# An output projection by one level of Strassen's algorithm, with sums of the weights made ahead of time on GpSimd

## The chip, the cores and the metric

The kernel runs on one core of one Trainium2 chip. The core has five engines with their own instruction streams: TensorE (PE, matmuls; PEld are its weight loads), VectorE (DVE), ScalarE (ACT), GpSimd (POOL) and SyncE (SP, which here issues all DMA transfers). The engines meet only through semaphores. The metric is the time of one execution on the device in microseconds (us); a lower one is better.

## The reference, cut to what matters

One layer of a hybrid decoder over 1024 positions of width 1024. The input is normalised and modulated, projected by w_in, and goes through three groups of heads (an mLSTM over chunks, a sliding-window attention, a stick-breaking attention), each gated by its own z. The three results stand side by side and are projected by w_out, normalised, gated and added to x:

```python
def rmsnorm(x, g):
    xf = x.astype(jnp.float32)
    y = xf * lax.rsqrt(jnp.mean(xf * xf, axis=-1, keepdims=True) + EPS)
    return (y * g.astype(jnp.float32)).astype(x.dtype)

def hybrid_layer(x, c_act, ...):
    mod = c_act @ w_mod + b_mod
    shift, scale, gate = jnp.split(mod, 3, axis=-1)
    h = rmsnorm(x, g_pre) * (1.0 + scale[:, None]) + shift[:, None]
    proj = h @ w_in
    ...
    y_m = mlstm_branch(mu, mv, mi, mf, ...) * jax.nn.silu(mz)
    y_a = swa_branch(aq, ak, av, a_sinks) * jax.nn.silu(az)
    y_s = stickbreak_branch(sq, sk, sv) * jax.nn.silu(sz)
    y = jnp.concatenate([y_m, y_a, y_s], axis=-1) @ w_out
    return x + gate[:, None] * rmsnorm(y, g_post)
```

All inputs are float32. y and w_out are 1024 x 1024.

## The kernel before, in words

Every product of float32 matrices is made of three matmuls on operands that are split in two: a high part (a cast to the type that PE reads, on ACT) and a low part (the difference, on DVE or POOL), joined as high·high + low·high + high·low. `split` does this. Tiles are 128 partitions by up to 512 columns, one PSUM bank.

The stages, in order: the modulation and the normalised h with the projection of the mLSTM's input; the convolution `cu` (until about 92 us); the gate chain, in which the mLSTM's gate values go through DRAM (`d_m`, `d_wi`) and, beside it, the row `gacc` = silu(c)·w_gate is summed from eight loads `wg` (`gate_row`, lines 528 to 540) and taken through PE (`gate_sum`, `gbps`, line 548); the m loop, eight chunks of the mLSTM (from about 160 us); the window attention; the stick-breaking attention; and the output projection (from 453 us). In all stages before the last, PE's idle time is filled with the projections by w_in: a `Filler` puts matmuls of the next projection (`pd`, `ptav`) between those of the stage. The result y is held transposed, in eight tiles of 128 of its columns (dst_j) by 1024 positions, in two halves of positions. `gated` multiplies each by its gate; the first six tiles are stored in DRAM as a high and a low part (`d_yh`, `d_yl`), the last two (`ys`) stay on the chip.

PE's instructions run in the order of the code. On the other engines a scheduler places them by priorities and by its own estimates, so that the order there is not that of the code. All loads and stores are in SP's one queue, in its order; each waits there for its semaphores, and what stands behind waits with it.

The output projection before: `wo_load` (lines 1078 to 1081) brings w_out in eight chunks of 512 KB and splits them; `y_load` brings the y parts back into hh and hl; then `out_mm` (lines 1104 to 1111) does three matmuls for each of 8 row tiles of 128 positions, 2 halves of 512 columns and 8 chunks k of 128. For the first four row tiles k is the outer loop, over eight PSUM banks. `out_fin` takes squares from PSUM on ACT, multiplies by the gate row `gbc` on DVE, makes the power on POOL and scales and adds x on DVE (lines 1122 to 1131).

## Time and profile before

| | us |
|---|---|
| median of 3 runs | 551.35 (551.1 to 551.76) |
| profiled execution | 551.07 |
| its span, first to last instruction | 549.3 |
| PE busy | 523.7 (95%) |
| DVE busy | 332.8 (61%) |
| ACT busy | 250.5 (46%) |
| POOL busy | 220.3 (40%) |
| output projection, first to last start of a matmul | 453.29 to 542.66 |
| mean granted PE clock, as a share | 0.999 |

The views give, for an instruction: its start and duration in us, the engine, the line of the kernel, the operation, the tile written and the tiles read, the shapes, and in brackets how long the engine had been idle before it and what released it. "x3" at the end of a row of a timeline stands for three alike, whose times are added. DMA issues are rows of SP's queue (SPq); their duration is that of the issue, not of the transfer.

### The profile page before, as it was taken

What the parts mean: (1) busy time and instruction counts of PE and PEld (TensorE: products, weight loads), DVE (VectorE), ACT (ScalarE), POOL (GpSimd) and SP (SyncE); (2) the same over time, 40 slices, a digit from 0 to 9 for tenths busy, and PEclk for the clock granted to TensorE, in tenths of its full rate; (3) what the DMA queues carried; (4) which work ended last, traced back from release to release, by engine and by line L of the source; (5) the groups of instructions that cost most, each with busy time, mean ns of one, the idle gap of its engine ahead of it and who ended that gap; (6) DMA issues with size and microseconds to landing.
All of it is one profiled execution on the core that took longest, in us unless ns stands there. A gap on an engine that the chain in (4) does not pass through costs nothing.

```text
span 549.3 us, 8550 instructions
## 1 busy us (share of the span) xinstructions
PE 523.7 (95%) x2953; PEld 448.3 (82%) x2953; DVE 332.8 (61%) x750; ACT 250.5 (46%) x571; POOL 220.3 (40%) x206
## 2 busy tenths in 40 slices
PE   4799999999999999999998999899999999999995
PEld 3577899999978989888786888788888888888884
DVE  4686692054726787678887489787868442118232
ACT  5643533361122333167587478667668332213111
POOL 2365765430023343244434348575666442111000
PEclk9999999999999999999999999999999999999999
DMA  8982361248986355699952488354421169607421
GB/s 299 417 308 71 116 233 51 58 146 237 279 247 209 107 159 138 162 277 269 235 178 88 145 225 248 134 153 154 135 78 58 39 201 401 239 1 243 141 85 68
DMA packets 63660, 96.57 MB, mean 176 GB/s; under 512 B 17601, under 2 KB 36993, under 8 KB 63489
## 3 DMA queue, kind: packets, MB, share of 16 engines
q1 hardware_dynamic: 63616, 96.03, 55.5%
q8 instruction: 23, 0.38, 0.3%
q14 instruction: 21, 0.16, 0.1%
HBM read 69.24 MB, written 25.20 MB: 172 GB/s over the span
## 4 chain that ended last, share of the span: by engine, by line
PE 79%; DVE 10%; DMA 3%; ACT 3%; issue 2%; SPq 1%; POOL 1%; DVEq 0%; POOLq 0%; ACTq 0%
PE pd L359 26%; PE ptav L385 6%; PE mu L233 6%; PE op L1111 5%; PE op L1110 5%; PE op L1109 5%; PE tp L996 3%; PE ptmif L385 2%; DVE cu L509 2%; DMA mbc<-d_m 2%; PE ops L1014 2%; PE ops L1015 2%; PE z L965 2%; PE mr L197 1%; PE z L966 1%
## 5 line engine op out<-in xcount | busy, mean ns | idle before, releaser
L359 PE MATMUL pd<-hh,wl_d 128*128 128x512 f32 x256 | 71.2, 400 | 0.0
L359 PE MATMUL pd<-hh,wh_d 128*128 128x512 f32 x256 | 70.6, 400 | 0.0
L359 PE MATMUL pd<-hl,wh_d 128*128 128x512 f32 x256 | 70.6, 398 | 0.0
L359 PEld LDWEIGHTS pd<-hh,wh_d 128*128 128x128 f32 x256 | 46.1, 188 | 8.4 <-issue 0.5
L359 PEld LDWEIGHTS pd<-hl,wh_d 128*128 128x128 f32 x256 | 46.1, 188 | 8.1
L302 POOL TENSOR_TENSOR wl_d<-w_d,wh_d 128x512 fp32r<-128x512 f32 x32 | 44.1, 1400 | 21.1 <-ACT wh_d L300 20.0
L359 PEld LDWEIGHTS pd<-hh,wl_d 128*128 128x128 f32 x256 | 45.8, 188 | 7.7
L1109 PE MATMUL op<-woh,hh 128*128 128x512 f32 x128 | 50.6, 396 | 0.0
L1110 PE MATMUL op<-woh,hl 128*128 128x512 f32 x128 | 50.6, 396 | 0.0
L1111 PE MATMUL op<-wol,hh 128*128 128x512 f32 x128 | 50.6, 396 | 0.0
L984 POOL TENSOR_TENSOR sg<-sg,pr 128x512 f32<-128x512 f32 (+1 forms) x30 | 31.1, 1043 | 20.8 <-DVE pr L982 20.6
L859 POOL TENSOR_SCALAR zb<-zb,mx 128x256 f32<-128x256 f32 (+1 forms) x24 | 21.6, 916 | 42.2 <-DVE mx L856 27.9
L70 ACT CAST ah<-tp 128x512 fp32r<-128x512 f32 (+2 forms) x56 | 24.3, 436 | 29.2 <-PE tp L996 21.2
L71 DVE TENSOR_TENSOR al<-tp,ah 128x512 fp32r<-128x512 f32 (+2 forms) x56 | 27.4, 493 | 16.9 <-ACT ah L70 16.4
L1122 ACT ACTIVATE sj<-op 128x512 f32<-128x512 f32 x16 | 9.5, 598 | 50.8 <-PE op L1111 48.3
L1110 PEld LDWEIGHTS op<-woh,hl 128*128 128x128 f32 x128 | 24.0, 188 | 5.9
L1111 PEld LDWEIGHTS op<-wol,hh 128*128 128x128 f32 x128 | 24.0, 188 | 5.8
L1109 PEld LDWEIGHTS op<-woh,hh 128*128 128x128 f32 x128 | 24.0, 188 | 5.7
L1126 POOL TENSOR_TENSOR st<-st,mhalf 128x1 f32<-128x1 f32 x8 | 4.9, 608 | 57.0 <-DVE st L1125 57.0
L849 ACT ACTIVATE zb<-zb,mx 128x256 f32<-128x256 f32 (+1 forms) x48 | 23.2, 486 | 7.3 <-DVE mx L838 7.3
L982 DVE TENSOR_TENSOR_SCAN pr<-z,mzero 128x128 f32<-128x128 f32 (+3 forms) x32 | 25.6, 814 | 0.4 <-ACT z L973 0.2
L971 ACT ACTIVATE sg<-z 128x512 f32<-128x512 f32 (+3 forms) x48 | 23.8, 495 | 1.3 <-PE z L968 1.1
(247 smaller groups left out, 1326.8 us busy)
## 6 DMA issues: line engine op xcount, KB each, us to landing
wm<-in_w_ss_dram SPq DMA_DIRECT2D x16, 512.0 KB, 7.8
w_d<-in_w_dm_dram SPq DMA_DIRECT2D x16, 512.0 KB, 3.7
xt<-in_x_dram SPq DMA_DIRECT2D x8, 512.0 KB, 8.3
wg<-in_w_gate_dram SPq DMA_DIRECT2D x8, 512.0 KB, 6.0
wo<-in_w_out_dram SPq DMA_DIRECT2D x8, 512.0 KB, 5.4
xr<-in_x_dram SPq DMA_DIRECT2D x8, 512.0 KB, 4.9
out_dram<-ot SPq DMA_DIRECT2D x16, 256.0 KB, 2.3
hh<-d_yh SPq DMA_DIRECT2D x12, 256.0 KB, 6.0
```

What stands on the lines that cost most here:

```text
L70: e_hi(dst_h, src)
L71: e_lo.tensor_tensor(out=dst_l, in0=src, in1=dst_h.bitcast(F32), op=ALU.subtract)
L233: T.matmul(mu_acc[j][n], w[:, cs], h[:, k, t], start=(k == 0 and w is wh and h is hh), stop=(k == KT - 1 and h is hl))
L302: G.tensor_tensor(out=wl[:, a:b], in0=z[:, a:b], in1=wh.bitcast(F32)[:, a:b], op=ALU.subtract)
L359: T.matmul(ps, w[:, k, :], h[:, k, t], start=(k == 0 and w is wh and h is hh), stop=(k == KT - 1 and h is hl))
L385: T.matmul(ps[:, 0:self.N], h[:, k, t], w[:, k % 2, :], start=(k == 0 and q == 0), stop=(k == KT - 1 and q == 2))
L971: A.activation(sg[:, 0:w], zps[:, 0:w], AF.Sigmoid)
L982: V.tensor_tensor_scan(out=rev(pr), data0=rev(zps), data1=mzero[:, 0:1].to_broadcast([P, w]), initial=1.0 if nxt is None else nxt, op0=ALU ...
L984: (G if w > 256 and (h > 0 or i > 3) else V).tensor_tensor(out=sg[:, 0:w], in0=sg[:, 0:w], in1=pr[:, 1:w + 1], op=ALU.mult)
L1109: T.matmul(o, hh[:, k, t], woh[:, k, cs], start=(k == 0), stop=False)
L1110: T.matmul(o, hl[:, k, t], woh[:, k, cs], start=False, stop=False)
L1111: T.matmul(o, hh[:, k, t], wol[:, k, cs], start=False, stop=(k == KT - 1))
```

## The change

The output projection becomes one level of Strassen's algorithm in Winograd's form. y and w_out are cut into quarters (positions by 512 for y, 512 by 512 for w_out). Seven products of quarters or sums of quarters take the place of eight. Each has 4 row tiles, 4 chunks of 128 and three matmuls of 128x512. Their names in the code are "11", "21", "t2", "t1", "22", "t3" and "t4", by the weights that they use, in this order. The weights t1 to t4 are sums of quarters of w_out; `w_sums` makes them in the gate chain's stage on POOL, in the room of the tile `mup` (the convolution's input, no longer needed there): for each of four chunks c it loads two rows of w_out (512 KB each), makes four differences, four casts and four low parts, and stores eight tiles of 256 KB in `d_th` and `d_tl`. The sums of y are made on DVE in the last stage (`y_ready`) from a third copy of y, `d_y`, in float32; `gated` now stores it for six tiles, and leaves out the split for the second half of four of them.

In `product` the row tile is the outer loop and the chunk the inner one. The results are added up in SBUF from PSUM by DVE (`e2` to `e4`); squares are now of the sum in SBUF. The x rows are loaded in halves. The loads of `bias_a`, `ka` and `va` (the window attention's) come after the work of w_sums on SP's queue.

The core of the diff:

```diff
+                store(d_y[dst_j, :, t], y)
+                if n == 1 and dst_j < 4:
+                    return
...
+    def w_sums():
+        room = mup.rearrange("p a b -> p (a b)")
+        z = room[:, 0:2 * D].rearrange("p (r a b) -> p r a b", r=2, a=2)
+        w11, w12, w21, w22 = z[:, 0, 0, :], z[:, 0, 1, :], z[:, 1, 0, :], z[:, 1, 1, :]
+        for c in range(4):
+            load(z[:, 0], w_out[c].rearrange("p (a b) -> p a b", a=2))
+            load(z[:, 1], w_out[4 + c].rearrange("p (a b) -> p a b", a=2))
+            for o, a, b in ((w11, w12, w11), (w12, w22, w12), (w22, w22, w11), (w21, w22, w21)):
+                G.tensor_tensor(out=o, in0=a, in1=b, op=ALU.subtract)
+            for m, (n, o) in enumerate(((0, w11), (2, w12), (1, w22), (3, w21))):
+                h = room[:, 2 * D + m % 2 * 512:2 * D + m % 2 * 512 + 512].bitcast(F32R)
+                split(h, o.bitcast(F32R), o, G.tensor_copy, G)
+                store(d_th[n, :, c, :], h)
+                store(d_tl[n, :, c, :], o)
...
     m_load(0)
+    w_sums()
...
-    woh = wop.tile([P, KT, D], F32R, name="woh")
-    wol = wop.tile([P, KT, D], F32R, name="wol")
-
-    def wo_load(k):
-        w = wop.tile([P, D], F32, tag="wo", bufs=2, name=f"wo{k}")
-        load(w, w_out[k])
-        split(woh[:, k, :], wol[:, k, :], w, A.copy, V if k % 2 else G)
...
+    def y_quarter(i, r, c):
+        if r == 1 and c >= 2:
+            return ys[:, c - 2, halves[i]]
+        if (i, r, c) in ahead:
+            return ahead.pop((i, r, c))
+        z = wop.tile([P, 512], F32, tag="yo", bufs=8, name=f"yo{i}{r}{c}")
+        load(z, d_y[4 * r + c][:, halves[i]])
+        return z
+    def w_pair(name):
+        wq_[name] = [wop.tile([P, 4, 512], F32R, tag=z, bufs=2, name=f"{z}{name}") for z in ("wqh", "wql")]
+        return wq_[name]
+    def w_ready(name, r, n):
+        h, l = w_pair(name)
+        for c in range(4):
+            z = wop.tile([P, 512], F32, tag="wo", bufs=4, name=f"wo{r}{n}{c}")
+            load(z, w_out[4 * r + c][:, halves[n]])
+            split(h[:, c, :], l[:, c, :], z, A.copy, V)
+    def t_ready(n):
+        h, l = w_pair(f"t{n}")
+        load(h, d_th[n - 1])
+        load(l, d_tl[n - 1])
+    def y_ready(i, r, chunk):
+        for c in range(4):
+            k = 4 * r + c
+            split(hh[:, k, halves[i]], hl[:, k, halves[i]], chunk(c), A.copy, V)
...
+    w_ready("11", 0, 0)
+    w_ready("21", 1, 0)
+    ahead.update({q: y_quarter(*q) for q in [(1, 0, 0), (1, 1, 0), (1, 0, 1), (1, 1, 1), (1, 0, 2), (1, 0, 3),
+                                             (0, 0, 0), (0, 0, 1)]})
     fill.through(I_SZ1)
     y_load(0)
-    for k in range(4, KT):
-        wo_load(k)
     fill.through(99)
     y_load(1)
+
...
+    def product(yi, yr, w, evac):
+        wh, wl = wq_[w]
+        ps = [fbank(f"p{w}_{i}") if i == 3 else ops_.tile([P, 512], F32, tag="op", name=f"p{w}_{i}")
+              for i in range(4)]
+        for i in range(4):
+            t = slice(yi * 512 + i * P, yi * 512 + (i + 1) * P)
+            for c in range(4):
+                k = 4 * yr + c
+                T.matmul(ps[i], hh[:, k, t], wh[:, c, :], start=(c == 0), stop=False)
+                T.matmul(ps[i], hl[:, k, t], wh[:, c, :], start=False, stop=False)
+                T.matmul(ps[i], hh[:, k, t], wl[:, c, :], start=False, stop=(c == 3))
+            evac(i, ps[i])
...
+    def square(src, i, n):
+        sj = op_.tile([P, 512], F32, tag="sj", bufs=2, name=f"sj{i}_{n}")
+        A.activation(sj, src, AF.Square, accum_out=st[:, i, n:n + 1])
+    def finish(i, parts):
+        xr = [wop.tile([P, 512], F32, tag="yo", bufs=8, name=f"xr{i}_{n}") for n in range(2)]
         for n in range(2):
+            load(xr[n], x[i * P:(i + 1) * P, halves[n]])
+        s_ = st[:, i, :]
+        V.tensor_scalar(out=s_[:, 2:3], in0=s_[:, 1:2], scalar1=s_[:, 0:1], scalar2=D * EPS, op0=ALU.add, op1=ALU.add)
+        G.tensor_tensor(out=s_[:, 3:4], in0=s_[:, 2:3], in1=mhalf[:, 0:1], op=ALU.pow)
+        for n, o, gate in parts:
+            if gate:
+                V.tensor_tensor(out=o, in0=o, in1=gbc[:, halves[n]], op=ALU.mult)
+        for n, o, _ in parts:
+            V.scalar_tensor_tensor(out=o, in0=o, scalar=s_[:, 3:4], in1=xr[n], op0=ALU.mult, op1=ALU.add)
+            store(out[i * P:(i + 1) * P, halves[n]], o)
+    def e1(i, ps):
+        A.copy(u1[i], ps)
+    def e2(i, ps):
+        V.tensor_tensor(out=o11[i], in0=ps, in1=u1[i], op=ALU.add)
+        square(o11[i], i, 0)
+        V.tensor_tensor(out=o11[i], in0=o11[i], in1=gbc[:, halves[0]], op=ALU.mult)
+    def e6(i, ps):
+        V.tensor_tensor(out=u1[i], in0=ps, in1=u1[i], op=ALU.add)
+    def e5(i, ps):
+        V.tensor_tensor(out=u3[i], in0=ps, in1=u1[i], op=ALU.add)
+    def e3(i, ps):
+        o = op_.tile([P, 512], F32, tag="o12", bufs=2, name=f"o12_{i}")
+        V.tensor_tensor(out=o, in0=ps, in1=u3[i], op=ALU.add)
+        square(o, i, 1)
+        finish(i, ((1, o, True), (0, o11[i], False)))
+    def e7(i, ps):
+        V.tensor_tensor(out=u1[i], in0=ps, in1=u1[i], op=ALU.add)
+        V.tensor_tensor(out=u3[i], in0=ps, in1=u3[i], op=ALU.add)
+        square(u3[i], 4 + i, 1)
+        V.tensor_tensor(out=u3[i], in0=u3[i], in1=gbc[:, halves[1]], op=ALU.mult)
+    def e4(i, ps):
+        V.tensor_tensor(out=u1[i], in0=u1[i], in1=ps, op=ALU.subtract)
+        square(u1[i], 4 + i, 0)
+        finish(4 + i, ((0, u1[i], True), (1, u3[i], False)))
...
-    for k in range(KT - 1):
-        for i in range(4):
-            for n in range(2):
-                out_mm(i, n, k)
...
+    product(0, 0, "11", e1)
+    t_ready(2)
+    y_ready(0, 0, lambda c: summed(yc(c), yc(c), y_quarter(0, 0, c), ALU.subtract))
+    product(0, 1, "21", e2)
+    t_ready(1)
+    y_ready(0, 1, lambda c: summed(yc(c), y_quarter(0, 1, c), yc(c), ALU.subtract))
+    product(0, 0, "t2", e6)
+    w_ready("22", 1, 1)
+    def s3(c):
+        z = y_quarter(0, 0, c)
+        return summed(z, z, y_quarter(1, 0, c), ALU.subtract)
+    y_ready(0, 0, s3)
+    product(1, 0, "t1", e5)
+    t_ready(3)
+    product(0, 1, "22", e3)
+    t_ready(4)
+    product(0, 0, "t3", e7)
+    product(1, 1, "t4", e4)
```

The change moves instructions on engines whose order the scheduler sets. Three places, each before and after.

SP's queue in the gate chain's stage: `wg` are the eight loads of w_gate, `vsh` and `vsl` the high and low parts of the projection `ptav` on their way to `d_v`, two for each of eight row tiles. Before, from the fifth wg to the eighth:

```order
L64 DMA wg_1358<-in_w_gate_dram 128x1024
L64 DMA d_v<-vsh_1394 768x1x64
L64 DMA d_v<-vsl_1395 768x1x64
L64 DMA wg_1361<-in_w_gate_dram 128x1024
L64 DMA d_v<-vsh_1425 768x1x64
L64 DMA wg_1364<-in_w_gate_dram 128x1024
L64 DMA d_v<-vsl_1426 768x1x64
L64 DMA wg_1367<-in_w_gate_dram 128x1024
```

After, the same stretch:

```order
L64 DMA wg_1449<-in_w_gate_dram 128x1024
L64 DMA d_v<-vsl_1486 768x1x64
L64 DMA d_th<-mup 128x512 x2
L64 DMA d_v<-vsh_1516 768x1x64
L64 DMA d_tl<-mup 128x512
L64 DMA d_v<-vsl_1517 768x1x64
L64 DMA wg_1452<-in_w_gate_dram 128x1024
L64 DMA d_tl<-mup 128x512
L64 DMA wg_1455<-in_w_gate_dram 128x1024
L64 DMA mup<-in_w_out_dram 128x1024
L64 DMA wg_1458<-in_w_gate_dram 128x1024
```

Four stores of w_sums and one of its loads now stand between the fifth and the eighth wg, and the sixth comes after the low part of row tile 4 (vsl_1517) where it came after that of row tile 3 (vsl_1395). Two more stores stand ahead of the fifth.

POOL in the m loop: `e` are the masks, `sm` the powers of a chunk, `cu` the scaling. Before, from the mask of chunk 1:

```order
L645 AFFINE_SELECT e_1634<-e_1634 128x512
L302 TENSOR_TENSOR wl_d_1689<-w_d_1640,wh_d_1688 128x512 x2
L746 TENSOR_TENSOR cu<-cu,col 128x3x128
L645 AFFINE_SELECT e_1722<-e_1722 128x512
L746 TENSOR_TENSOR cu<-cu,col 128x3x128
L732 TENSOR_TENSOR sm_1675<-sm_1675,mhalf 128x4
```

After, a piece of the same loop, from the power of chunk 0 to that of chunk 1:

```order
L757 TENSOR_TENSOR sm_1766<-sm_1766,mhalf 128x4
L70 CAST mup<-mup 128x512
L559 TENSOR_TENSOR mup<-mup 128x512 x2
L70 CAST mup<-mup 128x512
L771 TENSOR_TENSOR cu<-cu,col 128x3x128
L669 AFFINE_SELECT e_1907<-e_1907 128x512
L559 TENSOR_TENSOR mup<-mup 128x512
L71 TENSOR_TENSOR mup<-mup 128x512
L757 TENSOR_TENSOR sm_1863<-sm_1863,mhalf 128x4
```

From the mask of chunk 1 to the power of chunk 2, 14 operations of w_sums (those on mup) now stand in POOL's order.

SP's queue ahead of the output projection: before, two of the eight chunks of w_out and then the y parts:

```order
L64 DMA wo_5097<-in_w_out_dram 128x1024
L64 DMA wo_5101<-in_w_out_dram 128x1024
L64 DMA hh<-d_yh 128x512 x3
L64 DMA hl<-d_yl 128x512 x3
```

After, the last ten of sixteen loads of w_out and d_y, and the first of the y parts:

```order
L64 DMA yo_5215<-d_y 128x512
L64 DMA yo_5217<-d_y 128x512
L64 DMA wo_5195<-in_w_out_dram 128x512
L64 DMA yo_5219<-d_y 128x512
L64 DMA wo_5199<-in_w_out_dram 128x512
L64 DMA yo_5221<-d_y 128x512
L64 DMA wo_5203<-in_w_out_dram 128x512
L64 DMA yo_5223<-d_y 128x512
L64 DMA yo_5225<-d_y 128x512
L64 DMA wo_5207<-in_w_out_dram 128x512
L64 DMA hh<-d_yh 128x512
L64 DMA hl<-d_yl 128x512
```

Six loads of the same two kinds stand ahead of these. The y parts (hh, hl) come after all sixteen.

56 lines of the change are left out of this document (17 added, 39 removed).

## The prediction

> **What bounds the kernel now.** I read the page first, for the busy shares and the chain of work that ended last:
>
> ```profile
> span 549.3 us, 8550 instructions
> PE 523.7 (95%) x2953; PEld 448.3 (82%) x2953; DVE 332.8 (61%) x750; ACT 250.5 (46%) x571; POOL 220.3 (40%) x206
> PE 79%; DVE 10%; DMA 3%; ACT 3%; issue 2%; SPq 1%; POOL 1%; DVEq 0%; POOLq 0%; ACTq 0%
> ```
>
> TensorE (PE) sets the time almost everywhere. So a matmul that goes is a gain in full, but only while the others still deliver in time; work given to POOL, DVE or the DMA engines costs nothing until PE waits for it. The change takes matmuls out at the end and puts POOL and DMA work into a stage far ahead of it, so I read both stages by windows and instruction by instruction. First the output projection:
>
> ```profile
> 460.00:480.00 20.00, 20.00 (x87) 16.09 (x87) 3.64 (x2) 3.72 (x4) 4.24 (x2) 1.00 0.79 297
> 520.00:540.00 20.00, 20.00 (x87) 16.11 (x86) 5.84 (x10) 2.75 (x8) 1.10 (x2) 1.00 0.23 79
> 453.29 0.40 PE L1109 MATMUL op<-woh,hh 128*128 128x512 f32 x1
> 542.66 0.40 PE L1111 MATMUL op<-wol,hh 128*128 128x512 f32 x1
> ```
>
> The columns are the length of the stretch, then the busy time of PE, PEld, DVE, ACT and POOL: PE is full and the others are far from it. From the first to the last of 384 matmuls there are 383 steps: (542.66 − 453.29) / 383 = 0.2333 us each. After it comes the tail, from the timeline of the other engines:
>
> ```profile
> 543.15 0.60 ACT L1122 ACTIVATE sj<-op 128x512 f32<-128x512 f32 x1 [4.56 <-PE op L1111]
> 543.87 0.21 DVE L1125 TENSOR_SCALAR st<-st 128x1 f32<-128x1 f32 x1 [4.55 <-ACT sj L1122]
> 544.23 0.55 POOL L1126 TENSOR_TENSOR st<-st,mhalf 128x1 f32<-128x1 f32 x1 [10.64 <-DVE st L1125]
> 544.00 0.68 DVE L1127 TENSOR_TENSOR ot<-op,gbc 128x512 f32<-128x512 f32 x1
> 544.81 1.42 DVE L1130 SCALAR_TENSOR_TENSOR ot<-ot,st,xr 128x512 f32<-128x512 f32 x2
> ```
>
> PE ends at 542.66 + 0.40 = 543.06; square, sum, power and the two scalings end at 546.23; the last store closes the span 3.07 us later. The tail is 6.24 us.
>
> **Term 1, the matmuls: −11.2.** Seven products of 4 row tiles, 4 chunks and 3 matmuls are 336, against 384. 48 × 0.2333 = 11.2 us, of the same shape, so the pitch carries over.
>
> **Term 2, the start of the first product: +3.7.** Before, every bank needs only chunk 0 of y and w_out to begin. Now row tile 0 of the first product runs through all four chunks before row tile 1, and the two reloads per chunk stand behind 16 loads of 256 KB that were not there or came later.
>
> ```profile
> 442.59 1.72 SPq L64 DMA_DIRECT2D wo<-in_w_out_dram  x2
> 444.64 1.27 SPq L64 DMA_DIRECT2D hh<-d_yh  x3
> 450.00:455.00 5.00, 5.00 (x24) 4.10 (x23) 3.17 (x5) 1.74 (x3) 2.32 (x2) 1.00 0.99 355
> 452.00:456.00 4.00, 4.00 (x19) 3.27 (x18) 2.17 (x4) 1.25 (x3) 1.54 (x1) 1.00 1.05 401
> 456.00:460.00 4.00, 4.00 (x19) 3.23 (x18) 0.82 (x2) 1.67 (x2) 1.84 (x2) 1.00 1.05 414
> ```
>
> The last two columns are the DMA engines' share and GB/s: they are already full from 452 on, at 401 to 414. Up to chunk 3 there are now 16 + 8 loads of 256 KB, 6.29 MB; at 405 GB/s that is 15.5 us. From 442.6, with about 1 us to begin, the last piece lands at 459.1. PE comes to that piece after 9 matmuls, at 453.3 + 2.1 = 455.4. The stall is 459.1 − 455.4 = 3.7 us. Bounds: 0 if the loads find their room some 4 us earlier (nothing in the windows shows it), 5.9 at the 355 GB/s of 450 to 455 (17.7 us). The Trainium skill, "DMA: Bandwidth & Descriptors", Specifications, gives a limit of about 358 GB/s of HBM for one core; by it the loads would take 17.6 us and the stall would be 5.8. The rows above with 401 and 414 GB/s speak against it here, so my sum keeps 405.
>
> The other six products have their sums of y, weight splits and T loads behind 11.2 us of PE each: five to eight DVE operations of 0.7 us, and 2 MB of T, 5.2 us at 405 GB/s. I cost them at 0; were that cover gone, one late T load costs up to 3 us.
>
> **Term 3, the tail: +2.3.** A row tile that is finished now goes through an addition out of PSUM, a square of the sum, then the old chain: 0.68 for the addition in front of 546.23 − 543.15 = 3.08 us and a hop, about 4.0 us in a row, where PE delivers a row tile in 12 × 0.2333 = 2.8 us. DVE orders these mostly tile by tile, so in product "22" it falls behind by 1.2 us a tile, catches up some in "t3" and falls behind again in "t4". Walked instruction by instruction with the durations above, the last scaling ends 5.5 us after the last matmul instead of 3.2: the tail grows by 2.3 us. Bounds: +0.7 if the chains overlap fully (only the addition is new), +4 if none of the backlog is caught up.
>
> **Term 4, the gate row: +3.9.** w_sums puts 8 loads of 512 KB and 32 stores of 256 KB into SP's queue, 12.6 MB, a part of it among the loads of w_gate (wg). Their consumer and its end:
>
> ```profile
> DVE gacc L539 <- DMA wg<-in_w_gate_dram: 3.4, 6, 1.0
> 135.37 0.59 SPq L64 DMA_DIRECT2D wg<-in_w_gate_dram  x1
> 137.53 0.55 DVE L71 TENSOR_TENSOR vsl<-ptav,vsh 128x384 fp32r<-128x384 f32 x1
> 140.41 0.60 SPq L64 DMA_DIRECT2D wg<-in_w_gate_dram  x1
> 135.00:140.00 5.00, 5.00 (x30) 5.00 (x29) 3.79 (x5) 0.48 (x1) 0.00 (x0) 1.00 1.02 302
> 140.00:145.00 5.00, 5.00 (x31) 5.00 (x30) 3.55 (x4) 0.69 (x2) 0.00 (x0) 1.00 1.10 364
> 146.15 1.28 DVE L539 SCALAR_TENSOR_TENSOR gacc<-wg,csil,gacc 128x1024 f32<-128x1024 f32 x1 [0.23 <-DMA wg<-in_w_gate_dram]
> 148.79 1.45 PE L548 MATMUL gbps<-gacc,ones 128*128 128x512 f32 x3
> ```
>
> Six of the seven accumulations wait for their own load, the last at 146.15, and the DMA share is 1.02 and 1.10: nothing is free there. The sum ends at 147.43 and PE wants it at 148.79. Between the first and the last wg there now lie six stores of 256 KB and one load of 512 KB more, 2.1 MB, 5.1 us at 405 GB/s: the last wg comes at about 151.2, the sum ends at 152.5, PE begins at 152.7, +3.9. The queue alone gives less: wg5, issued at 135.37, now stands behind the store of the vsl made at 137.53, so wg5 goes out near 139, wg7 near 142.4 instead of 140.41, +2 for PE's 1.3 of slack, about +1. At 302 GB/s instead of 405 it is +5.7. I take 3.9, since the waits on DMA are what the rows show. Behind this wait on PE stands the next projection, so nothing is done meanwhile.
>
> **Term 5, the m loop: −0.5.** From 149 us on, bias_a and the ka and va loads are gone from SP's queue, and the loads of chunk 1 can start sooner. Two PE waits of that time are on the list:
>
> ```profile
> PE sps L693 <- ACT q L677: 0.6, 1, 0.6
> PE nps L715 <- DVE am L695: 0.5, 1, 0.5
> ```
>
> Both may vanish, −1.1. Against it, the last two rounds of w_sums run beside the first chunks; I set 0.6 for that, from the rows of the second rival.
>
> In gated(), 12 stores are added, 8 stores, 4 casts on ACT and 4 subtractions on POOL removed. No wait for them stands on PE's list of waits: 0.
>
> **Sum:** −11.2 + 3.7 + 2.3 + 3.9 − 0.5 = −1.8. The profiled run took 551.07 (span 549.3 and 1.77 around it), so 549.3; the median of the three runs shown is 0.28 above it: 549.5.
>
> **Rival 1, faster: the gate row does not wait.** If the stores slip behind the wg loads at the DMA engines, or the first rounds of w_sums are late enough for it, term 4 is near +1 (the bound by the queue alone): 546.6. If the first product's loads come in time too, 542.9. For it: the 1.3 us of slack, and 302 to 364 GB/s where 414 has been seen. Against it: the share above 1.
>
> **Rival 2, slower: POOL becomes the bound of the m loop.** w_sums is 32 subtractions and 16 casts of 128x512 on POOL.
>
> ```profile
> 150.74 2.54 POOL L550 TENSOR_TENSOR gbc<-gbc,rowb 128x512 f32<-128x512 f32 x2 [20.87 <-DVE gbc L549]
> 161.23 0.64 POOL L645 TENSOR_SCALAR_AFFINE_SELECT e<-e 128x512 f32<-128x512 f32 x1 [7.96 <-DVE e L644]
> 189.71 1.01 POOL L732 TENSOR_TENSOR sm<-sm,mhalf 128x4 f32<-128x4 f32 x1 [0.56 <-DVE sm L731]
> 182.94 0.56 DVE L735 TENSOR_TENSOR hn<-num,sm 128x384 f32<-128x384 f32 x1
> 185.02 0.49 PE L744 MATMUL yps<-ident,hn 128*128 128x128 f32 x3
> 195.00:200.00 5.00, 4.94 (x35) 4.13 (x34) 4.93 (x13) 1.21 (x2) 2.91 (x4) 1.00 0.80 233
> ```
>
> A subtraction takes 1.27 us; a cast lies between the one-input 0.64 and 1.27, I take 0.95: 48 operations, 56 us. From the mask of chunk 1 (161.23) to the power of chunk 2 (it ends at 190.72), 29.5 us, 14 of them stand in POOL's order, about 16 us, beside 10 us of the loop's own (a weight split of 2.5, three scalings, masks, powers): 26 of 29.5. DVE is at 4.93 of 5 there, and the engines slow each other:
>
> ```profile
> 447.71 2.41 POOL L71 TENSOR_TENSOR wol<-wo,woh 128x1024 fp32r<-128x1024 f32 x1 [3.37 <-DMA wo<-in_w_out_dram]
> 447.89 2.77 DVE L71 TENSOR_TENSOR hl<-ys,hh 128x512 fp32r<-128x512 f32 x1 [3.94 <-PE pd L359]
> ```
>
> A DVE operation of 0.69 takes 2.77 beside POOL's. From the point where the power (sm) is more than 1.5 us late (hn ends at 183.50, PE takes it at 185.02), each chunk costs PE the rest: about 2.1 us (2.77 − 0.69) in each of three chunks, 6.3 where I set 0.6: 549.5 + 5.7 = 555.2. Against it: POOL has 20.87 us of idleness ahead of 150.74 in which half of the rounds fit.
>
> **Rival 3, slower: the waits cost the clock.** Terms 2 and 4 leave PE idle for nearly 4 us each; the longest single wait that the list has after the start is 1.6.
>
> ```profile
> PE mu L233 <- ACT hh L219: 1.6, 1, 1.6
> 547.00:548.00 1.00, 0.00 (x0) 0.00 (x0) 0.00 (x0) 0.00 (x0) 0.00 (x0) 0.91 0.84 316
> 548.00:549.30 1.30, 0.00 (x0) 0.00 (x0) 0.00 (x0) 0.00 (x0) 0.00 (x0) 0.50 0.00 0
> ```
>
> After PE's end at 543.06 the granted clock (third column from the end) holds until about 547.9, 4.8 us, and then is 0.50. A wait over 4.8 us would thus be followed by matmuls at half speed; if they last as long as the fall took, it loses 2.4 us, two of them 4.8: 554.3. At 3.7 and 3.9 us my waits stay under it. The Trainium skill, "TensorE: Matmul & The Clock Gate", Part 1 ("What's actually happening"), says that the clock halves after an idle window of about 3.4 us that runs freely, so that a wait of 3.4 to 6.8 us may or may not meet it. The trace's 4.8 us lies inside that, and by the page the two waits could already trip it.
>
> **How the numbers follow.** The forecast has 0.42, with a range of its own of 546.9 to 552; rival 1 0.24; rival 2 0.24; rival 3 0.07; that T loads or splits of the later products come late (549.5 + 3) 0.03. The range for 8 in 10 goes from 542.5 (rival 1 with both loads in time) to 556 (rival 2). A difference of 0.2%, 1.1 us, is about what a measurement of this kernel can tell from none: 550.25 to 552.45 is "same". The forecast gives 0.28 faster, 0.11 same and 0.03 slower; rival 1 all of its 0.24 faster, rivals 2 and 3 and the late loads 0.34 less 0.02 same and 0.02 faster: 0.54, 0.13, 0.33.
>
> **What would show it.** Right: 336 matmuls 0.233 apart; a PE wait of 3 to 5 us on a DMA of hh or hl at the first product; one of 3 to 5 us at gbps, ended by DVE gacc, itself by DMA wg; a tail near 8.5 us; no new wait of over 1 us at yps. Wrong: no wait at gbps (rival 1); waits at yps on DVE hn, ended by POOL's power (rival 2); a granted clock below 1 in the windows after 153 or 459 (rival 3); waits of later products on T or on splits.

## The result: 20.8 us slower, and the profile after

| | before | after |
|---|---|---|
| median, us | 551.32 | 572.11 (570.67 to 574.18, 4 runs) |
| ratio to before | | 1.0381, interval 1.0353 to 1.041 |
| profiled execution, its span | 551.07, 549.3 | 571.60, 569.8 |

The forecast was 549.5 with a range of 542.5 to 556. Both the sign and the range were wrong. The page of the changed kernel, the lines that answer to the first ones shown of before:

```profile
span 569.8 us, 8753 instructions
PE 519.0 (91%) x2905; PEld 442.7 (78%) x2905; DVE 378.3 (66%) x818; ACT 258.2 (45%) x591; POOL 262.7 (46%) x246
PE 61%; DMA 11%; DVE 10%; POOL 6%; issue 4%; ACT 3%; SPq 2%; DVEq 0%; POOLq 0%; ACTq 0%
```

The 48 matmuls are gone, but PE is busy only 4.7 us less: some of the others ran at half speed. In the chain that ended last, DMA went from 3% to 11% and POOL from 1% to 6%. Where the time went, by the start of the same PE instruction in both traces:

| first start of | before | after | later by |
|---|---|---|---|
| last ptav (projection beside the gate chain) | 148.6 | 152.0 | 3.4 |
| gbps | 148.8 | 156.7 | 7.9 |
| qps (the m loop begins) | 161.4 | 171.1 | 9.7 |
| yps, chunk 0 | 176.9 | 186.7 | 9.8 |
| yps, chunk 1 | 185.0 | 204.6 | 19.6 |
| yps, chunk 2 | 193.2 | 214.3 | 21.1 |
| az (window attention) | 230.7 | 251.8 | 21.1 |
| first matmul of the last stage | 453.3 | 480.2 | 26.9 |
| last matmul | 542.7 | 560.6 | 17.9 |
| end of the span | 549.3 | 569.8 | 20.5 |

Three steps up, of 9.7, 11.4 and 5.8 (0.8 of the last lies ahead of the last stage, 5.0 is a wait), one down of 9.0 over the matmuls, and 2.6 in the tail. PE's waits in the changed kernel that the kernel before does not have (its one at yps was 0.7), the largest four, with the total, the number and the longest:

```profile
PE yps L769 <- DVE hn L760: 10.3, 2, 9.6
PE p L1175 <- DMA hh<-d_yh: 5.0, 1, 5.0
PE gbps L572 <- DVE gacc L545: 4.3, 1, 4.3
PE ptav L388 <- DVE vsl L71: 1.7, 1, 1.7
```

**The gate row.** The timeline of SP, DVE and PE, and then the windows (the clock is the third number from the end):

```profile
145.03 0.74 SPq L64 DMA_DIRECT2D wg<-in_w_gate_dram  x1
147.47 0.71 SPq L64 DMA_DIRECT2D wg<-in_w_gate_dram  x1
155.31 1.28 DVE L545 SCALAR_TENSOR_TENSOR gacc<-wg,csil,gacc 128x1024 f32<-128x1024 f32 x1 [1.53 <-DMA wg<-in_w_gate_dram]
156.65 3.67 PE L572 MATMUL gbps<-gacc,ones 128*128 128x512 f32 x4 [4.28 <-DVE gacc L545]
156.00:157.00 1.00, 0.35 (x1) 0.35 (x2) 0.59 (x1) 0.48 (x1) 1.00 (x1) 0.83 1.16 262
157.00:160.00 3.00, 3.00 (x5) 1.16 (x4) 1.25 (x2) 0.00 (x0) 0.53 (x2) 0.50 1.03 308
160.00:161.00 1.00, 1.00 (x5) 0.71 (x4) 0.65 (x1) 0.00 (x0) 1.00 (x2) 0.97 1.19 329
```

The last load of w_gate is issued at 147.47 where it was 140.41, 7.1 us later, and its consumer starts at 155.31 where it was 146.15, 9.2 later. So 7.1 of the delay is SP's queue and only 2.1 the transfer itself. PE waits 4.3 us, and when it begins again the granted clock has fallen to 0.50 for some 3.5 us, which makes another 1.8. (Of the 7.9 us in the table, 0.6 stand already at PE's first projection, ahead of any work of the sums: the two profiled executions differ by that at their start.)

**The m loop.** SP, POOL and PE around chunk 1, and two windows:

```profile
183.59 0.42 SPq L64 DMA_DIRECT2D d_tl<-mup  x1
189.05 0.35 SPq L64 DMA_DIRECT2D mup<-in_w_out_dram  x1
193.55 2.60 POOL L559 TENSOR_TENSOR mup<-mup 128x512 f32<-128x512 f32 x2 [8.33 <-DMA mup<-in_w_out_dram]
200.85 1.53 POOL L757 TENSOR_TENSOR sm<-sm,mhalf 128x4 f32<-128x4 f32 x1
204.64 0.90 PE L769 MATMUL yps<-ident,hn 128*128 128x128 f32 x3 [9.61 <-DVE hn L760]
197.00:199.00 2.00, 0.00 (x0) 0.00 (x0) 0.00 (x0) 0.54 (x2) 2.00 (x4) 0.65 0.37 139
199.00:207.00 8.00, 2.36 (x7) 1.97 (x8) 5.95 (x13) 1.58 (x5) 7.70 (x9) 0.50 0.28 99
```

This is one chain. The tile mup has room for one round, so the load of the next round waits in SP's queue until the stores of the round before have landed (183.59 to 189.05). POOL has a subtraction of that load next in its order and stands still for 8.33 us. Behind it, in the same order, stands the power `sm` of chunk 1, which the mLSTM needs; its last input is there at 191.0, but it comes at 200.85, and PE waits 9.6 us for what follows from it. Had POOL not stood still, the operations between (193.55 to 200.85) would have ended 8.3 us earlier, at about 192.5, and the power would be some 1.5 us late instead of 9.8; that is an estimate from these rows. The clock is at 0.50 when PE begins again.

**The last stage.** PE at the first product, the window behind it, and DVE's last row:

```profile
480.22 0.77 PE L1175 MATMUL p<-wqh,hh 128*128 128x512 f32 x1 [4.98 <-DMA hh<-d_yh]
478.00:484.00 6.00, 3.78 (x9) 2.36 (x9) 5.08 (x9) 1.35 (x3) 4.45 (x1) 0.50 1.03 392
565.44 1.41 DVE L1202 SCALAR_TENSOR_TENSOR u<-u,st,xr 128x512 f32<-128x512 f32 x2 [0.44 <-POOL st L1197]
```

PE waits 5.0 us for y. From the first to the last matmul it takes 80.4 us where 335 steps of 0.2333 are 78.2: the missing 2.2 are the half clock. The tail is 569.8 − 560.98 = 8.8 us where it was 6.24.

### The profile page after: what moved, and what is told of

It reads as the page before. It is cut to its first block, busy times and chain, and to the rows that moved or that the text cites. A ratio compares the mean times of both kernels' runs of the same rounds, so it can differ in the third digit from the quotient of the medians.

```text
span 569.8 us, 8753 instructions
## 1 busy us (share of the span) xinstructions
PE 519.0 (91%) x2905; PEld 442.7 (78%) x2905; DVE 378.3 (66%) x818; ACT 258.2 (45%) x591; POOL 262.7 (46%) x246
## 4 chain that ended last, share of the span: by engine, by line
PE 61%; DMA 11%; DVE 10%; POOL 6%; issue 4%; ACT 3%; SPq 2%; DVEq 0%; POOLq 0%; ACTq 0%
PE pd L362 20%; PE mu L236 6%; DMA d_tl<-mup 3%; PE tp L1021 3%; DMA wg<-in_w_gate_dram 3%; PE pt L1175 2%; PE pt L1177 2%; PE pt L1176 2%; SPq L64 2%; DVE cu L515 2%; PE p L1175 2%; PE p L1176 2%; PE p L1177 2%; DMA mup<-in_w_out_dram 2%; PE ptav L388 2%
## 5 line engine op out<-in xcount | busy, mean ns | idle before, releaser
L1197 POOL TENSOR_TENSOR st<-st,mhalf 128x1 f32<-128x1 f32 x8 | 7.1, 884 | 74.1 <-DVE st L1196 74.1
L559 POOL TENSOR_TENSOR mup<-mup 128x512 f32<-128x512 f32 x16 | 20.5, 1281 | 30.9 <-DMA mup<-in_w_out_dram 30.7
L1175 PE MATMUL pt<-wqht,hh 128*128 128x512 f32 x64 | 25.3, 396 | 0.0
L1176 PE MATMUL pt<-wqht,hl 128*128 128x512 f32 x64 | 25.3, 396 | 0.0
L1177 PE MATMUL pt<-wqlt,hh 128*128 128x512 f32 x64 | 25.3, 395 | 0.0
L1175 PE MATMUL p<-wqh,hh 128*128 128x512 f32 x48 | 19.8, 413 | 5.0 <-DMA hh<-d_yh 5.0
L998 ACT ACTIVATE z<-z 128x512 f32<-128x512 f32 (+3 forms) x48 | 24.0, 500 | 0.0
L388 PE MATMUL ptav<-wh_av,hh 128*128 128x384 f32 x64 | 22.0, 344 | 1.7 <-DVE vsl L71 1.7
```

Of the source, the lines that this page charges most:

```text
L388: T.matmul(ps[:, 0:self.N], h[:, k, t], w[:, k % 2, :], start=(k == 0 and q == 0), stop=(k == KT - 1 and q == 2))
L998: A.activation(zps[:, 0:w], zps[:, 0:w], AF.Sigmoid, scale=-1.0)
L1175: T.matmul(ps[i], hh[:, k, t], wh[:, c, :], start=(c == 0), stop=False)
L1176: T.matmul(ps[i], hl[:, k, t], wh[:, c, :], start=False, stop=False)
L1177: T.matmul(ps[i], hh[:, k, t], wl[:, c, :], start=False, stop=(c == 3))
```

## Experiments

All times are medians with the ratio to the kernel before on the same chip (550.8 to 551.5 us).

### With the sums and without them

One kernel leaves w_sums out of the changed kernel, the other adds it to the kernel before, whose last stage stays as it was.

```diff
 e1_no_sums, against the changed kernel
-    w_sums()
...
-        load(h, d_th[n - 1])
-        load(l, d_tl[n - 1])
+        load(h.rearrange("p (a b) n -> p a (b n)", a=2), d_yh[4:6].rearrange("a p n -> p a n"))
+        load(l.rearrange("p (a b) n -> p a (b n)", a=2), d_yl[4:6].rearrange("a p n -> p a n"))

 e2_sums_alone, against the kernel before
     m_load(0)
+    w_sums()
```

> The changed kernel without w_sums: no loads, no work on GpSimd and no stores for the sums of w_out; the four T operands are loaded from the stored parts of y instead (same bytes), so four of the seven products have other numbers. Theory A (the loss of 21.9 us ahead of the output projection comes from w_sums alone, by its transfers and its place in the queues) and theory B (it comes from w_sums alone, by its work on GpSimd) both expect that loss to be gone: what stays is the end, -11.2 for the matmuls, +5.0 for the wait at the first product, +2.0 to 2.2 for the halved clock after it, +2.6 for the tail = -1.4, so about 549 to 550.5 us, and no wait over 1.5 us at gbps and yps. If a good part of the loss stays (over 556 us), it comes from the moved loads of bias_a, ka and va or the stores of d_y.

> The kernel before, with w_sums added and its result not used; the output projection is the old one. A and B: the whole loss ahead of the output projection is there, +18 to +24, so 569 to 576 us, with waits of 4 to 5 us at gbps and of 8 to 10 at yps of chunk 1. If the loss needs the other moves too, clearly less (under 562).

Without the sums: 551.49, ratio 1.0007 (0.9993 to 1.0021). The sums alone: 572.36, ratio 1.0392 (1.0365 to 1.0419). The two add up to the whole change within their intervals: +0.6 and +21.5, together 22.1, against +20.8. PE's waits, first those of the kernel without sums, where nothing is left at gbps and 0.7 at yps, then those of the sums alone:

```profile
PE p L1174 <- ACT wqh L70: 5.4, 1, 5.4
PE yps L768 <- DVE hn L759: 0.7, 1, 0.7
```

```profile
PE yps L765 <- DVE hn L756: 9.2, 2, 8.5
PE gbps L568 <- DVE gacc L541: 5.9, 1, 5.9
```

So w_sums costs the whole difference, and Strassen's form itself gains nothing as it is built here: its −11.2 go into the wait at its start, the clock behind that, and the tail.

### Transfers or work

One kernel keeps the 8 loads and 32 stores of w_sums and leaves out all its work on POOL; the other keeps the 48 POOL operations and leaves out the transfers.

```diff
 e3_transfers_alone, in w_sums
-            for o, a, b in ((w11, w12, w11), (w12, w22, w12), (w22, w22, w11), (w21, w22, w21)):
-                G.tensor_tensor(out=o, in0=a, in1=b, op=ALU.subtract)
...
-                split(h, o.bitcast(F32R), o, G.tensor_copy, G)
-                store(d_th[n, :, c, :], h)
+                store(d_th[n, :, c, :], o)

 e4_work_alone, in w_sums
-            load(z[:, 0], w_out[c].rearrange("p (a b) -> p a b", a=2))
-            load(z[:, 1], w_out[4 + c].rearrange("p (a b) -> p a b", a=2))
...
-                store(d_th[n, :, c, :], h)
-                store(d_tl[n, :, c, :], o)
```

> The changed kernel with w_sums reduced to its loads and its 32 stores (of quarters of w_out as loaded), without any work on GpSimd, so the T operands are not the sums. Theory A: the late gate row stays (+8 by gbps, with the clock), the wait at yps goes, since nothing on GpSimd waits for a load any more: 558 to 562 us. Theory B (the work on GpSimd): both waits go, 549 to 551.

> The changed kernel with w_sums reduced to its 48 operations on GpSimd, without loads and stores (T operands from the stored parts of y). Theory A: neither wait is there, 549 to 552 us. Theory B: GpSimd's 45 us of work hold up the powers of the m loop and slow VectorE, so that a wait of several us at yps stays, 556 to 565.

Transfers alone: 560.99, ratio 1.0186 (1.0152 to 1.022). Work alone: 561.94, ratio 1.02 (1.0174 to 1.0225). Each is a half of it, 9.5 and 10.5 us above the kernel without sums. That they add up to the whole (20.0 against 20.6) does not make them two separate parts of it: with the transfers alone the wait at yps is gone, with the work alone it is 2.8 at most, and the 9.6 of the whole needs both, POOL's work standing in order behind a late transfer. Each half has waits of its own. For the transfers alone PE is 5.3 us late at gbps, with waits of at most 1.7 us up to there; the accumulations keep their 1.28 us. For the work alone they don't. The group of the accumulation in both kernels (least, median and largest duration in ns), and DVE and POOL of the second:

```profile
L545 DVE SCALAR_TENSOR_TENSOR gacc<-wg,csil,gacc x7: 1284/1285/1286, 142.2 to 152.8; 128x1024 f32<-128x1024 f32 x7
```

```profile
L545 DVE SCALAR_TENSOR_TENSOR gacc<-wg,csil,gacc x7: 1269/1847/2204, 141.2 to 154.4; 128x1024 f32<-128x1024 f32 x7
145.15 0.55 DVE L71 TENSOR_TENSOR vsl<-ptav,vsh 128x384 fp32r<-128x384 f32 x1
145.62 3.94 DVE L545 SCALAR_TENSOR_TENSOR gacc<-wg,csil,gacc 128x1024 f32<-128x1024 f32 x2
146.22 2.25 POOL L557 TENSOR_TENSOR mup<-mup 128x512 f32<-128x512 f32 x1
148.44 4.50 POOL L71 TENSOR_TENSOR mup<-mup 128x512 fp32r<-128x512 f32 x2
```

Beside each other, a DVE operation of 1.28 us takes about 2.0 and a POOL operation of 1.27 takes 2.25: each runs while the other waits. `vsl`, one of whose inputs is in PSUM, keeps its 0.55 in the midst of it. This slowing has little part in the late gate row of the changed kernel: there the seven accumulations keep 1.28 us each, since POOL stands still for 15.6 us of that time, waiting for a load. The Trainium skill states such a rule, "SBUF — State Buffer", Terms: VectorE and GpSimd share a pair of ports under a lock that is held for a whole instruction; and "GPSIMD Engine Reference", 1. Specifications, names VectorE operations with two inputs in SBUF among those that meet it. Both agree with these rows.

### How many rounds of the sums

```diff
 e8_two_rounds, against the changed kernel
-        for c in range(4):
+        for c in range(2):
...
+        for c2 in (slice(0, 2), slice(2, 4)):
+            load(h[:, c2, :], d_th[n - 1][:, 0:2, :])
+            load(l[:, c2, :], d_tl[n - 1][:, 0:2, :])
```

> The changed kernel with only the first two of the four rounds of w_sums (T chunks 2 and 3 are read from chunks 0 and 1, so other numbers). Theory A: what costs 10 us in the m loop are rounds 3 and 4, whose loads are late behind the queue and hold GpSimd and with it the powers up; without them the wait at yps goes and the gate row stays late by some us: 557 to 563. If the wait at yps does not come from them: 568 to 572.

557.15, ratio 1.0111 (1.0092 to 1.013). Rounds 3 and 4, which run into the m loop, cost 572.1 − 557.2 = 15 of the 21 us. The waits of this kernel:

```profile
PE gbps L572 <- DVE gacc L545: 4.1, 1, 4.1
PE yps L769 <- DVE hn L760: 0.7, 1, 0.7
```

The wait at yps is back to the 0.7 of a kernel without sums, and the one at gbps is still there: the first two rounds make the one (4.1 of 4.3 us), the last two the other.

### The last stage by itself

The y parts are issued right behind the first four loads of w_out, and the first product has the chunk as its outer loop, as the kernel before; once with w_sums, once without.

```diff
 e5_start_order, against the changed kernel
     w_ready("11", 0, 0)
+    fill.through(I_SZ1)
+    y_load(0)
     w_ready("21", 1, 0)
...
+        if w == "11":
+            at = [(i, c) for c in range(3) for i in range(4)] + [(i, 3) for i in range(4)]

 e6_no_sums_start_order: the same, without w_sums as in e1_no_sums
```

> The changed kernel with the y parts (hh, hl) loaded right after the first four pieces of w_out, and the chunk as the outer loop in product 11, as the old projection had it. Theory of the start: the wait of 5.0 us at the first product and the halved clock behind it (about 2 us) come from the sixteen loads ahead and from the row tile's need of all chunks, so both go: 7 us less than the changed kernel, 564 to 566. Rival: VectorE, which is full from 470 to 484 us there, holds the splits of w_out and y up whatever the loads do; then under 3 us are gained.

> The same, without w_sums (T operands from the stored parts of y, other numbers in four products): the end stage alone with its start mended. Theory: 551.5 of the run without w_sums less 7: 543.5 to 546, so -11.2 for the matmuls shows up but for the longer tail. Rival (VectorE holds the start up): 548 to 551.

With the sums: 566.99, ratio 1.0273 (1.0238 to 1.0308), 5.1 below the changed kernel, where 7 had been expected. Without: 548.76, ratio 0.995 (0.9929 to 0.997), only 2.7 below the kernel without sums; it misses the 543.5 to 546 that were expected and lies in the range of the rival, that VectorE holds the start up. The rival's sign is not there, though: in both kernels the wait at the first product is gone; two new ones, for T, take its place. Of the kernel with the sums and then of the one without:

```profile
PE pt L1179 <- DMA wqlt<-d_tl: 1.7, 1, 1.7
PE pt L1177 <- DMA wqht<-d_th: 0.7, 1, 0.7
```

```profile
PE pt L1178 <- DMA wqlt<-d_yl: 2.4, 2, 1.7
```

Of the 11.2 us that the matmuls give, 2.4 go to T and 3.6 to the tail (9.9 after the last matmul, where it was 6.24); the profiled span is 4.0 shorter than before, the median 2.1. This kernel, whose T are other numbers, shows what the form gives when nothing is paid for the sums: a half per cent. It is no strict bound for a placing of the sums, since its last stage can still be made shorter: from its first matmul to the end of the span it takes 91.5 us, and 89.6 in the kernel "with room" below.

### The sums at other places

First, in the last stage itself: differences and low parts on POOL, from quarters of w_out. (In this kernel t3 has the opposite sign; the operations are the same in number and size.) Then on DVE right behind the convolution, where DVE is idle from 90 to 107 us before the change; T goes through DRAM once, in float32, and is split in the last stage on ACT and DVE, with the start mended as above.

```diff
 e7_sums_late, against e5_start_order
-    w_sums()
...
+    t1 = w_load(0, 1, t1s)
+    less(t1, t1, w11)
...
-    t_ready(2)
+    w_split("t2", t2, G)

 e10_sums_on_dve, against e5_start_order
     cvp_stk.close()
+    w_sums()
...
+            z = room if c % 2 else wsp.tile([P, 2, 2, 512], F32, tag="z", bufs=1, name=f"wz{c}")
+                V.tensor_tensor(out=o, in0=a, in1=b, op=ALU.subtract)
+            store(d_t[c], z.rearrange("p r a b -> p (r a) b"))
...
-        load(h, d_th[n - 1])
-        load(l, d_tl[n - 1])
+        for c in range(4):
+            split(h[:, c, :], l[:, c, :], t_f[n][:, c, :], A.copy, V)
```

> The start mended, and the sums of w_out made in the last stage: quarters loaded in float32, 16 subtractions and 16 low parts on GpSimd, 16 casts on ScalarE, nothing stored in DRAM; nothing of it in the gate chain or the m loop. Theory: GpSimd has 41 us of such work in 67 us in which it did nothing, and the time is that of the run without sums, 543 to 547. Rival: GpSimd's operations slow VectorE's (2.77 us for 0.69 has been seen) and the splits come late, waits of PE at later products, 549 to 556.

> The sums of w_out made on VectorE right behind the convolution, where it had nothing to do (0.0 to 0.3 of 5 us from 85 to 105 in the kernel before), in two buffers, kept in float32 in DRAM (4 stores of 1 MB, 8.4 MB moved instead of 12.6) and split in the last stage on ScalarE and VectorE (16 casts, 16 subtractions more there); the start of the last stage mended as before. Nothing of it is in GpSimd's queue, and its transfers stand ahead of the wg loads. If the loss is one of queues and of the hour, as theory A has it: no waits at gbps and yps, and the time is that of the run without sums and with the mended start, less its 2.4 us of waits on T: 544 to 549, faster than before. Rival: the transfers before 125 us make w_av or wg late all the same, or the extra splits make VectorE late in the last stage: 550 to 556.

In the last stage: 566.73, ratio 1.0284 (1.0264 to 1.0305). The gate row and the m loop are as before the change (gbps at 148.4), and nearly all of the loss lies between 475 and 500 us:

```profile
485.00:490.00 5.00, 2.23 (x4) 1.33 (x5) 5.00 (x5) 0.72 (x2) 5.00 (x4) 0.50 0.45 150
485.93 0.68 DVE L1206 TENSOR_TENSOR o<-p,u 128x512 f32<-128x512 f32 x1
489.28 1.75 DVE L1208 TENSOR_TENSOR o<-o,gbc 128x512 f32<-128x512 f32 x1
487.10 6.73 POOL L1115 TENSOR_TENSOR t2s<-t2s,wo 128x512 f32<-128x512 f32 x4
```

DVE and POOL are both busy for the whole of the window and get five and four operations done in 5 us: the same conflict, 1.75 for a DVE operation of 0.68, with the exception of the one that reads PSUM (`p`).

On DVE behind the convolution: 562.56, ratio 1.0205 (1.0182 to 1.0229). The gate row and yps are clean, and two other waits have come. PE's, then SP's rows of the two last loads of w_av (issued at 101.83 and 103.8 before the change), ACT's cast behind the first of them, and the window behind:

```profile
PE pt L1183 <- ACT hh L70: 5.1, 1, 5.1
PE ptav L388 <- DVE sl_ak L425: 4.8, 1, 4.8
110.19 0.38 SPq L64 DMA_DIRECT2D w_av<-in_w_av_dram  x1
112.73 0.43 SPq L64 DMA_DIRECT2D w_av<-in_w_av_dram  x1
115.72 0.83 ACT L303 CAST wh_av<-w_av 128x768 fp32r<-128x768 f32 x1 [11.54 <-DMA w_av<-in_w_av_dram]
120.00:125.00 5.00, 3.85 (x12) 3.34 (x11) 4.48 (x8) 3.91 (x6) 3.66 (x3) 0.50 0.28 109
```

The loads stand in SP's queue behind stores and loads of the sums that wait for DVE and for their buffers. What PE then waits for is again an engine that waits in order: ACT stands still for 11.5 us for w_av, and behind that cast stand its copies `sh_ak` out of PSUM, which `sl_ak` on DVE needs. In the last stage the split of t1 stands in DVE's order ahead of the sums of y that the third product needs. A variant gives the gate multiplications of `finish` to POOL:

```diff
 e11_gate_on_pool, against e10_sums_on_dve
-                V.tensor_tensor(out=o, in0=o, in1=gbc[:, halves[n]], op=ALU.mult)
+                G.tensor_tensor(out=o, in0=o, in1=gbc[:, halves[n]], op=ALU.mult)
```

> The same, and the eight multiplications by the gate row in the finishing of a row tile go from VectorE to GpSimd, which is idle there. Theory: VectorE has 3.0 us of work per row tile there against 2.8 of TensorE, 2.3 without it, so the backlog and 1 to 3 us of the tail go. Rival: GpSimd's 1.28 us lie in the chain (square, sum, power wait behind them) and slow VectorE's operations: no gain or up to 2 us lost.

564.44, ratio 1.0237 (1.0213 to 1.0261): nothing won, the intervals of the two overlap.

Last, the two waits of the sums on DVE are taken away by what makes them wait: room of their own for two rounds, ten buffers for y in place of eight and the split of t1 behind the sums of y; and then also `wqk_s`, the load that was late in its place.

```diff
 e12_room_for_loads, against e10_sums_on_dve
+    ws_stk = ExitStack()
+    wsp = pool("wsp", side="right", stack=ws_stk)
     cvp_stk = ExitStack()
...
-            z = room if c % 2 else wsp.tile([P, 2, 2, 512], F32, tag="z", bufs=1, name=f"wz{c}")
+            z = room if c == 2 else wsp.tile([P, 2, 2, 512], F32, tag="z", bufs=2, name=f"wz{c}")
...
-    t_ready(1)
     y_ready(0, 1, lambda c: summed(yc(c), y_quarter(0, 1, c), yc(c), ALU.subtract))
+    t_ready(1)

 e13_wqk_early, against e12_room_for_loads
+    wq_stk = ExitStack()
+    wqk_s = pool("wqp", stack=wq_stk).tile([MD, 2, MH, MD], F32, name="wqk_s")
+    load(wqk_s, wqk)
     ws_stk = ExitStack()
...
-    wqk_s = Q("wqk_s", (MD, 2, MH, MD))
-    load(wqk_s, wqk)
```

> The sums as in the kernel 'sums on DVE' (stored in float32, split in the last stage), with three things changed: two buffers of their own, opened ahead of the convolution, so that three of the four rounds load without waiting for a store (the two last loads of w_av stand in SP's queue behind one such wait instead of three); two more buffers for y; the split of t1 behind the sums of y. Theory 'order': what the sums cost there (562.6 against 548.8 without sums) was waiting in SP's queue (PE wait at ptav of 4.8 and half clock behind it) and in DVE's order in the last stage (wait of 5.0 at the third product and half clock behind it); both vanish, and the time is 547 to 551: no PE wait of over 2 us at ptav, none at pt, clock 1.0 from 100 to 130 and from 480 to 500. Theory 'work': the 16 operations of DVE and 8.4 MB of transfers cost by themselves, wherever they wait: 556 to 562, with the waits moved to other places.

> As the run 'room for loads' (551.96), with one load moved: wqk_s (96x768) gets room of its own ahead of the convolution and is issued before the sums' loads, where it stood in SP's queue behind two stores that wait for DVE's sums. In that run PE waited 4.2 us for it at gmps, and the granted clock in the 5 us behind was 0.66, which is another 1.5 to 2 us. Theory 'order': that is the rest of what the sums cost, so no wait at gmps, clock 1.0 from 100 to 130, and 545 to 548, faster than before by 0.6 to 1.1%. Theory 'work': the wait moves to the next that needs DVE or a transfer there (ptav, whose w_av loads come behind the same stores), and the time stays at 550 to 552.

With room: 551.96, ratio 1.0019 (1.0002 to 1.0036), 10.6 below the kernel that it mends and just above the 551 that "order" had given as its upper end. With `wqk_s` early as well: 551.07, ratio 0.9999 (0.9984 to 1.0014). One wait of over 2 us is left in each, of the first and then of the second:

```profile
PE gmps L584 <- DMA wqk_s<-in_wqk_dram: 4.2, 1, 4.2
```

```profile
PE ptav L388 <- DVE sl_ak L425: 3.7, 1, 3.7
```

The wait of 5.1 us at the third product is gone in both (1.0 at most is left), as "order" had it; in the second the wait moved to ptav, whose loads are the next in the queue behind the sums' stores, as "work" had it: ACT again stands still for w_av, for 9.5 us. So most of what the sums cost on DVE is where they stand in the queues, since the same work and the same bytes cost 10.6 us less; the three changes of the first kernel were made together, and their shares are not known. The last 2 to 3 us above 548.8 were not removed. They are not all that the sums still cost: in the kernel with room gbps begins at 155.6, 6.8 us later than before the change, and its shorter last stage gives a part back. Whether another order of SP's queue would remove this stays open. Of the kernels with the sums none was faster than before.

## Why the prediction was wrong, step by step

| step | predicted | measured |
|---|---|---|
| Term 1, matmuls | −11.2 | −11.2 (48 fewer) |
| Term 2, start of the first product | +3.7 | +7.2: wait 5.0, half clock 2.2 |
| Term 3, tail | +2.3 | +2.6 |
| Term 4, gate row | +3.9 | +9.7: 7.9 by gbps, half clock 1.8 |
| Term 5, m loop | −0.5 | +11.4: wait 9.6, the rest mostly half clock |
| between the m loop and the last stage | 0 | +0.8 |
| sum | −1.8 | +20.5 |

**Term 5 failed**: +11.4 where −0.5 stood, 11.9 of the 22.3 us between the two sums. The sign would have been lost without it: terms 4 and 2 are off by 5.8 and 3.5, which alone turns −1.8 into a loss. The prediction looked for what POOL has to do (26 of 29.5 us) and set 0.6, since it fits (a cast even takes 0.61 with nothing beside it, not the 0.95 that was set). It named the right place in rival 2, `sm` late in POOL's order and `hn` behind it, but priced it by POOL's being busy. That was the small part (some 1.5 of the 9.8 us by which the power is late, as estimated above). For the rest POOL stood still for 8.3 us, waiting in order for a load that waited in SP's queue for stores to land, out of a tile with room for one round. That a late transfer on one engine's queue holds up unrelated work behind it was a question that the prediction asked of SP and not of POOL. The order of POOL that stood in the document showed both rows; the single room `mup` was in the diff. The kernel with two rounds and the one with the transfers alone, where the 9.6 are gone, show this; the price of 15 us for the last two rounds is larger than any rival's.

**Term 4 was mis-sized** and its two causes weighed the wrong way. "The queue alone gives less", +2 for the last wg; it was 7.1, and the transfer, taken as the main cause with 5.1 (2.1 MB at 405 GB/s are 5.2), was 2.1. In SP's queue a store also waits for the POOL operation that makes its data, and the prediction counted the stores' bytes, not their waits. Rival 1 was wrong throughout: there is a wait at gbps and one at the first product.

**Term 2 was a fair size but for the clock**: 5.0 inside the bounds of 0 to 5.9, and the experiment that mends the order removes the wait (with 5.1 won, 2.7 without the sums, where the wait and its clock make 7.2). It changes the order of the loads and the order of the loop together, and in the kernel without sums the profile ends the same wait with a cast of w_out and not with a load of y; so it is shown that the order makes the wait, and not which of its two parts does. The cover that was costed at 0 for T held almost: 2.4 us of waits once the start is mended. By the Trainium skill's limit of about 358 GB/s ("DMA: Bandwidth & Descriptors", Specifications) the stall was to be 5.8, which is nearer to 5.0 than 3.7 is, but not for that reason: the window at the wait shows 392 GB/s.

**Term 3 was right** (2.6 against 2.3), and so was term 1.

**Rival 3 was right in kind and its threshold was wrong.** The prediction read 4.8 us off the end of the program and kept its waits under it. In the changed kernel the clock fell during or at the end of all three large waits, of 4.3, 9.6 and 5.0 us, and the half clock costs about 1.8 + 1.6 + 2.2 = 5.6 us (the second is half of the 3.2 us from 204.6 until the clock is back). One fall at the end of a program is one sample. The statement of the Trainium skill that the prediction quoted, "TensorE: Matmul & The Clock Gate", Part 1 ("What's actually happening"), an idle window of about 3.4 us that runs freely, was the better guide. The traces agree with its length and that it runs freely (3.41 us, last section), but not with its being idle: in the window ahead of the fall at 197.6 PE was busy for 0.83 us.

## What to carry to other kernels

Work that is put on an idle engine is not free because it fits: ask for each new instruction what it waits for, and what stands behind it on that engine and on the queue that issues its transfers. Give such work its own buffers so that no load of it waits for a store of it, or put it where nothing behind it is due. A wait of PE from about 2 us on is to be costed with the clock behind it (1.6 to 2.2 us each in the changed kernel), and DVE work that reads two operands from SBUF at about 1.6 to 2.6 times its duration beside POOL work of the same kind, or 4 times as in the pair of rows that the prediction shows.

## What the runs showed of the hardware

**The clock falls by a fixed grid of 3.41 us, and so after waits of very different length.** With the work alone on POOL, a wait of 1.94 us was enough. PE and the windows there, and then two windows of the changed kernel's m loop (PE's busy time stands behind the length, the clock is the third number from the end):

```profile
89.72 0.47 PE L388 MATMUL ptmif<-wh_mif,hh 128*128 128x392 f32 x1 [1.94 <-ACT igf L450]
86.59:89.99 3.40, 1.46 (x8) 1.13 (x7) 0.00 (x0) 1.82 (x5) 3.40 (x3) 1.00 0.10 29
90.01:93.41 3.40, 3.40 (x12) 3.40 (x12) 0.09 (x1) 0.10 (x2) 3.40 (x3) 0.50 0.11 29
93.42:96.82 3.40, 3.40 (x21) 3.40 (x20) 0.00 (x0) 0.55 (x2) 3.40 (x4) 1.00 0.37 110
194.20:197.61 3.41, 0.83 (x8) 0.66 (x6) 1.50 (x1) 0.00 (x0) 3.33 (x4) 1.00 0.70 240
197.62:201.02 3.40, 0.00 (x0) 0.00 (x0) 1.13 (x3) 1.49 (x4) 3.40 (x5) 0.50 0.21 77
```

The clock is 0.50 from 90.0, when PE is at work again, until 93.4. In three other runs even a wait of 1.6 us near the start was followed by half clock, in the rest the same wait was not. The clock records of the 14 traces show why. Within a trace all changes of the clock up to PE's last matmul lie whole multiples of 3.41 us apart: the stretches at 0.50 last 3.41, 6.83, 10.24, 13.65 or 23.89 us. What counts is PE's work in such a window. All 21 windows at full clock in which PE was busy for less than 1.5 us were followed by half clock, and none with more than 1.9; in between both occur. Half clock ends after a window with at least 3.0 us of work. So the fall comes 1.5 to 5.0 us after PE's last matmul, by where the wait lies in the grid, and by these figures a wait of 3.8 us always brings it, as it leaves one window with less than 1.5 us of work wherever it begins (an estimate). The two waits of 3.7 and 3.9 us that the prediction had would hardly have escaped.

**DVE and POOL take turns where DVE reads two operands from SBUF**: 0.68 to 1.75 and 1.28 to 2.0 for DVE, 1.27 to 2.25 for POOL, and no change where an operand comes from PSUM (0.55 and 0.68). Operations that read one tile from SBUF can be held up too. In the changed kernel the first step of `gacc`, a tile times a scalar, took 1.85 beside a subtraction on POOL where it took 0.76 before, and a cast on POOL took 1.67 beside an accumulation where 0.61 has been seen:

```profile
137.14 1.85 DVE L543 TENSOR_SCALAR gacc<-wg,csil 128x1024 f32<-128x1024 f32 x1 [2.46 <-DMA wg<-in_w_gate_dram]
155.39 1.67 POOL L70 CAST mup<-mup 128x512 fp32r<-128x512 f32 x1
```

The prediction had taken one pair of rows (0.69 to 2.77) as the price of any DVE operation beside POOL.
